# Router tiles over the merged activations, nine expert slots, ten half-megabyte buffers and a written load order in a one-core encoder layer

## The chip, the core and the metric

The program runs on one core of a Trainium2 chip. The core has a matrix engine (PE; its weight loads are shown apart as PEld), a vector engine (DVE), a scalar engine (ACT), GpSimd (POOL) and a sync engine (SP) that here does nothing but issue DMA transfers. The metric is the device time of one execution in microseconds (us). Nearly all of the time goes into streaming weights from HBM once: 616 MB.

## The reference

One layer over 256 tokens of width 2048. Cut to what matters here:

```python
mod = silu(c) @ ada_w + ada_b                    # 2048 -> 6 x 2048
sh1, sc1, g1, sh2, sc2, g2 = split(mod, 6)
h = rmsnorm(x) * (1 + sc1) + sh1
q, k, v, u = split(h @ w_in)                     # 2048 -> 4096
y = gate_na * (attention(q, k, v) @ w_na) + gate_f * (fourier(u) @ w_f)
x = x + g1 * (y @ w_out)                         # w_out: 2048 x 2048, "mow" in the kernel
h = rmsnorm(x) * (1 + sc2) + sh2
group = argmax(h @ wg); two best of 8 experts in that group
x = x + g2 * sum(weight_e * (silu(h @ gate_e) * (h @ up_e)) @ down_e)     # 32 experts, 403 MB
out = rmsnorm(x) * final_g
```

All is float32. The experts' weights ("exw") are 192 pieces of 2 MB (2,097,152 bytes): eight groups ("quads") of four experts, each of 16 pieces gate/up and 8 pieces down.

## The kernel before, in words

**Dense front.** A `section` of a product loads 0.5 MB of weights into one of NW = 8 ring buffers (`load`, L100-104, queue of SP), splits it into a high part on ACT and a low part on DVE (`split`, L106-108) and makes three matmul passes, high with high, high with low, low with high (`t_part`, `n_part`). The high and low parts lie in six 4 KB buffers (`s4`, L89-90). Between the sections, further 0.5 MB loads of `ada2` go through the same ring; each is multiplied on DVE by the conditioning vector and added up (`ada_some`, `mac`, the rows "ada" of DVE). The first stage (L355-379) takes the input projection and half of the gates together with the 64 products of `ada1` (L215). Then come Fourier, output of Fourier, attention (eight 256 KB bias tiles, L495-497), the other gates, the output of attention; there the merged activations arise as `mh`, `ml` (high and low, four tiles each).

**Last dense product ("mow", L618-633).** Four column blocks of 512 with eight sections each. Only here does the code fix the order of SP's queue (`manual_schedule`); elsewhere a scheduler orders the instructions of every engine. In each step the code issues a mow load, then perhaps a quarter (0.5 MB) of one of the first five expert slots (`early_some`, 20 quarters in all, no ring buffer), then perhaps an ada load: 14 of the 23 that remain in the 32 steps (PACE), and nine (`late`) after them. After each column block `residual` (L597-602) multiplies the sum by g1, adds it to x1 and squares it for the norm; `router_part` (L604-616) transposes the new 512 columns of x1 and multiplies them by the router's weights into `plg`.

**Router (L634-702).** Opens new tiles. `lgs` and its neighbours lie at byte 170,880 and after it in each partition, where ring buffers lay before. It copies `plg` into `lgs` (L645-647), sums the squares (`sst`), forms 1/rms, turns the logits with a selecting matmul (`cst`, `lgs`), scales them (`lg`, L656), finds the best group and two experts (`onehot`, L667-674), ranks the tokens (`ma`, `rk`) and builds the 0/1 matrix `gt` that picks 32 tokens for each expert.

**Experts (`quad`, L760-817).** `gather` forms the picked tokens `hq` (`ph`); then each of 24 pieces is multiplied from its slot: 16 into `pg` and `pu`, 8 into `pd`. Pieces lie in slots of 2 MB: five early ones, two more and one that is used once (`NX` = 7, `slot`, `ring` L713-731), so eight at first, seven later, since the one used once becomes the output tile x2. A slot is loaded again, by SP, when PE has used it.

**Tail (L878-918).** The last piece is loaded in four parts; two halves of 256 columns go through `yb`, `po`, the sum with x2 and the square; then 1/rms, scaling and four output transfers.

Of the kernel before, what the change touches and what calls it, by code (L numbers as in the profile page):

```python
# [27 lines left out]
C_ID, C_LT, C_ONE, C_SELR, C_IOTA, C_DESC, C_THR, C_END = 0, 128, 256, 384, 420, 452, 484, 492  # L28
# [4 lines left out]
def const_table():  # L33
# [5 lines left out]
    for j in range(2):  # L39
        t[64 * j + np.arange(36), C_SELR + np.arange(36)] = 1  # L40
# [17 lines left out]
def build(tc, A, out, dbg=None):  # L58
# [15 lines left out]
    wp, _wp = pool("wp", "right", bufs=NW)  # L74
# [14 lines left out]
    def s4(shape, s, dt=F32):  # L89
        return r0.tile(shape, dt, tag="s4", bufs=6, name=nm(s))  # L90
# [8 lines left out]

    def load(src):  # L100

        w = wp.tile([P, 1024], F32, tag="w", name=nm("w"))
        nc.sync.dma_start(w, src)
        return w
# [75 lines left out]
    nc.gpsimd.dma_start(rb, A["rb"])  # L180
# [10 lines left out]
    for i in range(2):  # L191
        crow = wp.tile([P, 1024], F32, tag="w", name=nm("crow"))
# [212 lines left out]
    for i, c in ((0, 1024), (2, 512)):  # L405
        fr = wp.tile([P, 1024], F32, tag="w", name=nm("fr"))
# [5 lines left out]
    zh = rf.tile([P, 2, 258], F32R, name="zh")  # L412
    zl = rf.tile([P, 2, 258], F32R, name="zl")
# [70 lines left out]
    def attention(half):  # L484
# [9 lines left out]
        for i in range(4):  # L494
            bt = rb_.tile([P, 2, 2, P], F32, tag="bias", bufs=2, name=nm("bias"))  # L495
            nc.sync.dma_start(bt, A["rpb"][4 * half + i])
# [38 lines left out]
    _ra.close()  # L535
    mt, _mt = pool("mt", "right")
# [26 lines left out]
    nc.sync.dma_start(x1, A["x"])  # L563
# [20 lines left out]
    nc.vector.tensor_tensor(crow, pc[0:1, 0:36], rb, op=OP.add)  # L584
# [11 lines left out]
    def residual(cb, acs):  # L596
        c = slice(512 * cb, 512 * cb + 512)  # L597
        for tb in range(2):
# [3 lines left out]
            nc.scalar.activation(tmp, x1[:, tb, c], AF.Square, accum_out=ss2[:, tb, cb:cb + 1])  # L602

    def router_part(cb):  # L604
        for pr in range(2):
            px = mps()
            for i in range(2):
                kc = 4 * cb + 2 * pr + i
                for tb in range(2):
                    nc.tensor.transpose(px[:, T * i + P * tb:T * i + P * tb + P],  # L610
                                        x1[:, tb, kc * P:kc * P + P], ident)
            xt2 = s4([P, 2, T], "x1t")
            nc.scalar.copy(xt2, px.rearrange("p (a b) -> p a b", a=2))
            for i in range(2):
# [206 lines left out]
    for go in late:  # L821
        go()
# [172 lines left out]
```

## Time and profile before

| | |
|---|---|
| median of 3 runs | 1600.57 us (1597.12 to 1603.39) |
| the profiled execution | 1598.41 us, of it span 1596.6 us |
| PE, DVE, ACT, POOL busy | 77%, 43%, 22%, 3% |
| moved by DMA | 616.27 MB, mean 386 GB/s |
| chain that ended last | DMA 47%, PE 38%, DVE 5% |

How to read it: busy times are those of one execution; "w<-exw" is a slot (or a ring buffer) filled from the experts' weights; an arrow <- behind an idle time names what ended it. PEclk is the clock that PE was granted, as a share of 2.4 GHz. The dense front lasts to about 642 us, the router to about 670 us, the experts to the end.

### The profile page before, as it was taken

What the parts mean: (1) busy time and instruction counts of PE and PEld (TensorE: products, weight loads), DVE (VectorE), ACT (ScalarE), POOL (GpSimd) and SP (SyncE); (2) the same over time, 40 slices, a digit from 0 to 9 for tenths busy, and PEclk for the clock granted to TensorE, in tenths of its full rate; (3) what the DMA queues carried; (4) which work ended last, traced back from release to release, by engine and by line L of the source; (5) the groups of instructions that cost most, each with busy time, mean ns of one, the idle gap of its engine ahead of it and who ended that gap; (6) DMA issues with size and microseconds to landing.
All of it is one profiled execution on the core that took longest, in us unless ns stands there. A gap on an engine that the chain in (4) does not pass through costs nothing.

```text
span 1596.6 us, 20401 instructions
## 1 busy us (share of the span) xinstructions
PE 1233.2 (77%) x8430; PEld 745.9 (47%) x8430; DVE 679.3 (43%) x946; ACT 349.7 (22%) x535; POOL 43.6 (3%) x40
## 2 busy tenths in 40 slices
PE   4999999999999899679657567667567566556755
PEld 3989999999899777325112112112112112111111
DVE  6989999798887966603003002002002002002002
ACT  3543355444555343112000000000000000000002
POOL 0000000300002100000000000000000000000001
PEclk9999999999999999799889779789779889777878
DMA  9999999899997899699999999999999999999996
GB/s 360 389 337 339 352 359 365 273 328 369 329 346 267 318 409 380 261 427 426 427 426 427 428 427 426 427 426 427 426 427 428 427 427 426 417 427 426 425 428 280
DMA packets 89229, 616.27 MB, mean 386 GB/s; under 512 B 10037, under 2 KB 10341, under 8 KB 64937
## 3 DMA queue, kind: packets, MB, share of 16 engines
q1 hardware_dynamic: 87700, 611.10, 95.2%
q10 hardware_dynamic: 1252, 3.48, 0.6%
q8 instruction: 68, 1.11, 0.3%
q0 software_dynamic: 176, 0.31, 0.1%
q14 instruction: 33, 0.26, 0.0%
HBM read 611.71 MB, written 2.10 MB: 384 GB/s over the span
## 4 chain that ended last, share of the span: by engine, by line
DMA 47%; PE 38%; DVE 5%; issue 1%; ACT 1%; POOL 0%; DVEq 0%; POOLq 0%; ACTq 0%
DMA w<-exw 45%; PE acc L116 23%; PE pd L116 3%; PE m L116 2%; PE ph L116 2%; PE pg L116 2%; PE pu L116 2%; DMA w<-ada 2%; DVE lo L108 1%; DVE ada L223 1%; PE po L116 1%; PE at_u L116 1%; PE pr L116 0%; DVE t L600 0%; PE sp L116 0%
## 5 line engine op out<-in xcount | busy, mean ns | idle before, releaser
L116 PE MATMUL pg<-w,hq 128*32 128x512 f32 x1024 | 185.0, 777 | 217.0 <-DMA w<-exw 217.0
L108 DVE TENSOR_TENSOR lo<-w,hi 128x1024 fp32r<-128x1024 f32 x192 | 239.5, 1253 | 42.6 <-ACT hi L107 37.8
L107 ACT CAST hi<-w 128x1024 fp32r<-128x1024 f32 x192 | 200.8, 1051 | 229.2 <-PE acc L116 179.5
L790 DVE TENSOR_TENSOR act<-act,pu 128x512 f32<-128x512 f32 x8 | 5.5, 688 | 526.2 <-PE pu L116 526.2
L116 PE MATMUL acc<-hh,hi 128*128 128x256 f32 x768 | 212.1, 280 | 0.6 <-ACT hi L107 0.6
L116 PE MATMUL acc<-hl,hi 128*128 128x256 f32 x768 | 211.3, 278 | 0.0
L116 PE MATMUL acc<-hh,lo 128*128 128x256 f32 x768 | 205.7, 279 | 2.2 <-DVE lo L108 2.1
L116 PEld LDWEIGHTS pg<-w,hq 128*32 128x32 f32 x1024 | 25.0, 118 | 363.1 <-DMA w<-exw 345.3
L116 PE MATMUL pu<-w,hq 128*32 128x512 f32 x1024 | 190.0, 793 | 0.0
L223 DVE SCALAR_TENSOR_TENSOR ada<-w,condT,ada 128x1024 f32<-128x1024 f32 x124 | 162.1, 1314 | 13.1 <-DMA w<-ada 12.2
L116 PE MATMUL pd<-w,aT 128*32 128x512 f32 x1024 | 132.2, 630 | 37.0 <-DMA w<-exw 35.5
L116 PEld LDWEIGHTS acc<-hh,hi 128*128 128x128 f32 x768 | 145.3, 189 | 2.1 <-ACT hi L107 1.4
L116 PEld LDWEIGHTS acc<-hl,hi 128*128 128x128 f32 x768 | 145.1, 189 | 0.3 <-issue 0.2
L786 ACT ACTIVATE act<-pg 128x512 f32<-128x512 f32 x8 | 4.8, 597 | 637.3 <-PE pg L116 637.3
L116 PEld LDWEIGHTS acc<-hh,lo 128*128 128x128 f32 x768 | 141.2, 189 | 3.0 <-DVE lo L108 2.6
L116 PE MATMUL po<-yb,gwt 128*128 128x512 f32 (+1 forms) x132 | 75.0, 659 | 30.4 <-DVE yb L808 19.4
L116 PEld LDWEIGHTS pu<-w,hq 128*32 128x32 f32 x1024 | 43.0, 138 | 109.9 <-issue 108.2
L116 PEld LDWEIGHTS ph<-gt,x 128*128 128x128 f32 x512 | 65.2, 195 | 43.8 <-issue 25.6
L116 PEld LDWEIGHTS pd<-w,aT 128*32 128x32 f32 x1024 | 28.7, 112 | 114.7 <-issue 60.4
L215 DVE SCALAR_TENSOR_TENSOR w<-w,condR 128x1024 f32<-128x1024 f32 x64 | 77.7, 1219 | 9.1 <-ACT condR L197 7.4
L116 PE MATMUL ph<-gt,x 128*128 128x128 f32 x512 | 74.8, 288 | 7.1 <-ACT hq L756 3.5
L815 DVE TENSOR_TENSOR x<-x,po 128x512 f32<-128x512 f32 (+1 forms) x66 | 44.3, 671 | 79.8 <-PE po L116 79.8
(246 smaller groups left out, 1481.4 us busy)
## 6 DMA issues: line engine op xcount, KB each, us to landing
w<-exw SPq DMA_DIRECT2D x186, 2048.0 KB, 30.7
w<-ada SPq DMA_DIRECT2D x192, 512.0 KB, 5.8
w<-mixw SPq DMA_DIRECT2D x64, 512.0 KB, 5.6
w<-gatew SPq DMA_DIRECT2D x64, 512.0 KB, 5.4
w<-mow SPq DMA_DIRECT2D x32, 512.0 KB, 10.2
w<-exw SPq DMA_DIRECT2D x24, 512.0 KB, 10.2
w<-fow SPq DMA_DIRECT2D x16, 512.0 KB, 5.3
w<-now SPq DMA_DIRECT2D x16, 512.0 KB, 5.1
```

The source lines that it names most:

```text
L107: nc.scalar.copy(hi, src)
L108: nc.vector.tensor_tensor(lo, src, hi.bitcast(F32), op=OP.subtract)
L116: return nc.tensor.matmul(ps, lhsT, rhs, start=start, stop=stop, skip_group_check=True)
L215: nc.vector.scalar_tensor_tensor(w, w, 1.0, condR[:, 1024 * kh:1024 * kh + 1024], op0=OP.mult, op1=OP.mult, accum_out=dst)
L223: nc.vector.scalar_tensor_tensor(a, w, condT[:, kc:kc + 1], a, op0=OP.mult, op1=OP.add)
L786: nc.scalar.activation(at_[:, 0], pg, AF.Silu)
L790: nc.vector.tensor_tensor(at_[:, 1], at_[:, 0], pu, op=OP.mult)
L815: nc.vector.tensor_tensor(x2[:, tb, c], base[:, tb, c], po[:, 0:n], op=OP.add)
```

## The change

It has these parts:

1. The router's tiles (`rt2`) are opened on the other side of the memory, where `mh` and `ml` lay (bytes 117,216 to 133,696 of each partition); constants that are not needed after the front, and the `s4` tiles, get pools of their own that are closed with the ring.
2. NX is 8: nine expert slots at first, eight later.
3. The ring has ten buffers (NW 8, NQX 2) to the end of the gate sections before the last, eight after.
4. The order of SP's queue is as written from the gates on to the end of mow, not in mow alone. The bias tiles are loaded from GpSimd's queue, the load of x into x1 stands after mow's fifth section.
5. All 23 remaining ada loads go into mow's first 28 steps. Of the 20 early quarters seven go into the steps (one each fourth step), and 13 after the last mow load.
6. The router's logits are computed with tokens on partitions (stationary x1t, 36 columns of `wr`), so that neither `lgs` nor the turning matmul is needed; the very last square moves from ACT to DVE.
7. The experts' weights of the tokens, the row count and the second `gather` are issued after the first `gather`'s last eviction.
8. The last 512 columns of the last quad are multiplied 128 columns at a time, from pieces rearranged on the host; the last piece comes in three parts; only the last 256 columns are multiplied by the final gain after the norm. One output transfer goes through ACT's queue.
9. Tiles are padded so that their addresses agree modulo 64.

The diff, cut to its core:

```diff
-    wp, _wp = pool("wp", "right", bufs=NW)
+    cq, _cq = pool("cq", "right")
+    r4, _r4 = pool("r4", "right")
+    wp, _wp = pool("wp", "right")
+    wq, _wq = pool("wq", "right")
+    rings = [(wp, i) for i in range(NW)] + [(wq, i) for i in range(NW, NW + NQX)]
...
+    def half(s):
+
+        p, i = rings.pop(0)
+        rings.append((p, i))
+        return p.tile([P, 1024], F32, tag=f"w{i}", bufs=1, name=nm(s))
...
+
+    written = ExitStack()
+    written.enter_context(tc.manual_schedule(engines={nc.sync.engine}))
...
-            nc.sync.dma_start(bt, A["rpb"][4 * half + i])
+            nc.gpsimd.dma_start(bt, A["rpb"][4 * half + i])
...
+    rings[:] = [r for r in rings if r[0] is wp]
+    _wq.close()
...
-    nc.sync.dma_start(x1, A["x"])
...
-            nc.scalar.activation(tmp, x1[:, tb, c], AF.Square, accum_out=ss2[:, tb, cb:cb + 1])
+            if cb == 3 and tb:
+                nc.vector.scalar_tensor_tensor(tmp, x1[:, tb, c], 1.0, x1[:, tb, c], op0=OP.mult, op1=OP.mult,
+                                               accum_out=ss2[:, tb, cb:cb + 1])
+            else:
+                nc.scalar.activation(tmp, x1[:, tb, c], AF.Square, accum_out=ss2[:, tb, cb:cb + 1])
 
     def router_part(cb):
+
+        px = [mps() for _ in range(2)]
+        for tb in range(2):
+            for pr in range(2):
+                for i in range(2):
+                    kc = 4 * cb + 2 * pr + i
+                    nc.tensor.transpose(px[pr][:, T * i + P * tb:T * i + P * tb + P],
+                                        x1[:, tb, kc * P:kc * P + P], ident)
         for pr in range(2):
-            px = mps()
+            xt2 = s4([P, 2, T], "x1t")
+            nc.scalar.copy(xt2, px[pr].rearrange("p (a b) -> p a b", a=2))
             for i in range(2):
                 kc = 4 * cb + 2 * pr + i
                 for tb in range(2):
-                    nc.tensor.transpose(px[:, T * i + P * tb:T * i + P * tb + P],
-                                        x1[:, tb, kc * P:kc * P + P], ident)
-            xt2 = s4([P, 2, T], "x1t")
-            nc.scalar.copy(xt2, px.rearrange("p (a b) -> p a b", a=2))
-            for i in range(2):
-                kc = 4 * cb + 2 * pr + i
-                mm(plg[64 * i:64 * i + 36, 0:T], wra[:, kc, :], xt2[:, i, :], kc < 2, kc >= KC - 2)
-
-    with tc.manual_schedule(engines={nc.sync.engine}):
-        for cb in range(4):
-            acs = acc_tiles()
-            for s in range(8):
-                n_part(load(A["mow"][cb, s]), acs, mhf, mlf, 2 * s, s == 0, s == 7)
-                i = 8 * cb + s
-                early_some(max(0, i - 5) * 4 * NA // 26 - max(0, i - 6) * 4 * NA // 26)
-                ada_some((i + 1) * PACE // 32 - i * PACE // 32)
-                if s == 4 and cb:
-                    router_part(cb - 1)
-                if s == 4 and cb == 1:
-
-                    nc.scalar.activation(warm, ones[:, 0:1], AF.Sqrt)
-            if cb == 3:
-                late = [ada_load() for _ in range(len(ada_q))]
-            residual(cb, acs)
+
+                    mm(plg[:, 36 * tb:36 * tb + 36], xt2[:, i, tb * P:tb * P + P], wra[:, kc, :],
+                       kc == 0 and tb == 0, kc == KC - 1)
+
+    left = len(ada_q)
+    for cb in range(4):
+        acs = acc_tiles()
+        for s in range(8):
+            n_part(load(A["mow"][cb, s]), acs, mhf, mlf, 2 * s, s == 0, s == 7)
+            i = 8 * cb + s
+            ada_some(min(left, (i + 1) * left // 28) - (left - len(ada_q)))
+            if i == 4:
+                nc.sync.dma_start(x1, A["x"])
+            if i % 4 == 3 and i > 4:
+                early_some(1)
+            if s == 4 and cb:
+                router_part(cb - 1)
+            if s == 4 and cb == 1:
+
+                nc.scalar.activation(warm, ones[:, 0:1], AF.Sqrt)
+        if cb == 3:
+            early_some(len(quarters))
+        residual(cb, acs)
+    written.close()
...
+    for e in (_mt, _wp, _r4, _cq):
+        e.close()
+
+    rt, _rt2 = pool("rt2", reuse_waits="tile")
     wxb, _wxb = pool("wxb", reuse_waits="tile")
-    rt, _rt2 = pool("rt2", "right")
+    tp, _tp = pool("tp", "right", reuse_waits="tile")
...
-    lgs = rt.tile([P, T], F32, name="lgs")
-    nc.gpsimd.memset(lgs, 0.0)
-    for i in range(2):
-        nc.vector.tensor_copy(lgs[64 * i:64 * i + 36, :], plg[64 * i:64 * i + 36, 0:T])
     sst = rt.tile([P, 2], F32, name="sst")
     nc.vector.tensor_reduce(sst, ss2, axis=AX.X, op=OP.add)
     rs2 = rstd_of(rt, sst, 2)
-    pl = mps()
-    for tb in range(2):
-        mm(pl[:, 36 * tb:36 * tb + 36], lgs[:, tb * P:tb * P + P], cst[:, C_SELR:C_SELR + 36], True, True)
     lg = rt.tile([P, 2, 36], F32, name="lg")
     for tb in range(2):
-        nc.vector.scalar_tensor_tensor(lg[:, tb, :], pl[:, 36 * tb:36 * tb + 36], rs2[:, tb:tb + 1], cbr,
+        nc.vector.scalar_tensor_tensor(lg[:, tb, :], plg[:, 36 * tb:36 * tb + 36], rs2[:, tb:tb + 1], cbr,
                                        op0=OP.mult, op1=OP.add)
...
+            if q == NQ - 1 and cb == 3:
+
+                for k2 in range(2):
+                    w = get(A["exw"][q, KC + 2 * cb + k2], (2048, 4096) if tail is None or k2 == 0 else
+                            (2048, 3072, 4096))
+                    for i in range(2):
+                        c = slice(256 * k2 + 128 * i, 256 * k2 + 128 * i + 128)
+                        for kc in range(4):
+                            for j in range(4):
+                                mm(pd[32 * j:32 * j + 32, c], aT[:, kc * P + 32 * j:kc * P + 32 * j + 32],
+                                   w[4 * i + kc][:, P * j:P * j + P], kc == 0, kc == 3)
+                        if k2:
+                            down(cb, c, pd, yb)
+                    if k2 == 0:
+                        down(cb, slice(0, 256), pd, yb)
+                continue
...
+    behind, first_evict = ExitStack(), last_evict[0]
+    behind.enter_context(tc.issue_after(last_evict[0].ins))
+
+
+    nc.vector.tensor_tensor(ge, gl, gm[:, :, None].to_broadcast([P, 2, 4]), op=OP.subtract)
...
+        with tc.issue_after(first_evict.ins) if q == 0 else ExitStack():
+            hg = gather(q + 1, rk, q % 2)
...
         n = c.stop - c.start
-        nc.scalar.activation(s4([P, 512], "sq")[:, 0:n], x2[:, tb, c], AF.Square, accum_out=ss3[:, tb, i:i + 1])
-        if gain:
+        nc.scalar.activation(temp([P, 512], "sq")[:, 0:n], x2[:, tb, c], AF.Square,
+                             accum_out=ss3[:, tb, parts[tb]:parts[tb] + 1])
+        parts[tb] += 1
+        if c.start < LASTC:
             nc.gpsimd.tensor_tensor(x2[:, tb, c], x2[:, tb, c], fg[:, c], op=OP.mult)
...
-    nc.sync.dma_start(out[:, 0, c0], x2[:, 0, c0])
+    nc.scalar.dma_start(out[:, 0, c0], x2[:, 0, c0])
...
-NW, NX, NA = 8, 7, 5
-
-LEAD, PACE = 3, 14
+NW, NQX, NX, NA = 8, 2, 8, 5
+
+LASTC = 1792
```

What the order of the instructions shows at three places. DVE, around the end of the first column block of mow: t and x are the residual's product and sum, lo the low part of a section, ada an ada product. Before:

```order
L108 TENSOR_TENSOR lo_6467<-w_6464,hi_6466 128x1024
L600 TENSOR_TENSOR t_6483<-acc_6327,g1r_5907 128x512
L601 TENSOR_TENSOR x_6285<-x_6285,t_6483 128x512
L600 TENSOR_TENSOR t_6487<-acc_6328,g1r_5907 128x512
L108 TENSOR_TENSOR lo_6496<-w_6493,hi_6495 128x1024
L601 TENSOR_TENSOR x_6285<-x_6285,t_6487 128x512
L223 SCALAR_TENSOR_TENSOR ada_5950<-w_6531,condT,ada_5950 128x1024
L108 TENSOR_TENSOR lo_6515<-w_6512,hi_6514 128x1024
L108 TENSOR_TENSOR lo_6537<-w_6534,hi_6536 128x1024
L108 TENSOR_TENSOR lo_6555<-w_6552,hi_6554 128x1024
```

After:

```order
L116 TENSOR_TENSOR lo_6483<-w_6480,hi_6482 128x1024
L231 SCALAR_TENSOR_TENSOR ada_5962<-w_6498,condT,ada_5962 128x1024
L612 TENSOR_TENSOR t_6502<-acc_6336,g1r_5919 128x512
L613 TENSOR_TENSOR x_6297<-x_6297,t_6502 128x512
L612 TENSOR_TENSOR t_6506<-acc_6337,g1r_5919 128x512
L231 SCALAR_TENSOR_TENSOR ada_5962<-w_6530,condT,ada_5962 128x1024
L116 TENSOR_TENSOR lo_6515<-w_6512,hi_6514 128x1024
L613 TENSOR_TENSOR x_6297<-x_6297,t_6506 128x512
L116 TENSOR_TENSOR lo_6536<-w_6533,hi_6535 128x1024
L231 SCALAR_TENSOR_TENSOR ada_5962<-w_6569,condT,ada_5962 128x1024
```

One ada product (w_6530) now stands between the second t and the low part of the next block's first section. The same holds at the other two block boundaries.

DVE, from the last residual of mow towards the sum of squares (sst). Before (three more ada products follow, then sst):

```order
L600 TENSOR_TENSOR t_7068<-acc_6869,g1r_5907 128x512
L223 SCALAR_TENSOR_TENSOR ada_5950<-w_7052,condT,ada_5950 128x1024
L600 TENSOR_TENSOR t_7072<-acc_6870,g1r_5907 128x512
L601 TENSOR_TENSOR x_6285<-x_6285,t_7068 128x512
L223 SCALAR_TENSOR_TENSOR ada_5950<-w_7054,condT,ada_5950 128x1024
L601 TENSOR_TENSOR x_6285<-x_6285,t_7072 128x512
L223 SCALAR_TENSOR_TENSOR ada_5950<-w_7056,condT,ada_5950 128x1024
L223 SCALAR_TENSOR_TENSOR ada_5950<-w_7058,condT,ada_5950 128x1024
L223 SCALAR_TENSOR_TENSOR ada_5950<-w_7060,condT,ada_5950 128x1024
```

After:

```order
L612 TENSOR_TENSOR t_7098<-acc_6903,g1r_5919 128x512
L613 TENSOR_TENSOR x_6297<-x_6297,t_7098 128x512
L612 TENSOR_TENSOR t_7102<-acc_6904,g1r_5919 128x512
L613 TENSOR_TENSOR x_6297<-x_6297,t_7102 128x512
L615 SCALAR_TENSOR_TENSOR t_7102,ss_6334<-x_6297 128x512
L675 TENSOR_REDUCE sst<-ss_6334 128x2
```

The eight ada products that stood between and behind the residual's steps are gone from here, and a square (L615) has come.

SP, from the last mow load to the slots. Before, the last mow load and then:

```order
L103 DMA w_7030<-mow 128x1024
L572 DMA w_6297<-exw 128x1024
L103 DMA w_7049<-ada 128x1024
L103 DMA w_7052<-ada 128x1024
L103 DMA w_7054<-ada 128x1024
L103 DMA w_7056<-ada 128x1024
L103 DMA w_7058<-ada 128x1024
L103 DMA w_7060<-ada 128x1024
L103 DMA w_7062<-ada 128x1024
L103 DMA w_7064<-ada 128x1024
L103 DMA w_7066<-ada 128x1024
L727 DMA w_7327<-exw 128x4096
```

After:

```order
L111 DMA w_7066<-mow 128x1024
L584 DMA w_6305<-exw 128x1024 x2
L584 DMA w_6306<-exw 128x1024 x4
L584 DMA w_6307<-exw 128x1024 x4
L584 DMA w_6308<-exw 128x1024 x4
L748 DMA w_7351<-exw 128x4096
L748 DMA w_7361<-exw 128x4096
L748 DMA w_7371<-exw 128x4096
L748 DMA w_7381<-exw 128x4096
L748 DMA w_7391<-exw 128x4096
```

The nine ada loads stand ahead of the 2 MB slots (128x4096) in the kernel before; now 14 quarters of early slots stand there, the first of them that of the last step, and a fourth 2 MB slot follows directly.

## Rows read from the trace of the kernel before

**Rows 1.** The page: shares of the chain of waits by engine.

```profile
DMA 47%; PE 38%; DVE 5%; issue 1%; ACT 1%; POOL 0%; DVEq 0%; POOLq 0%; ACTq 0%
```

**Rows 2.** Windows by stage: start:end, length, busy per engine, granted clock, DMA share, GB/s.

```profile
0.00:100.00 100.00, 79.00 (x562) 71.51 (x563) 81.76 (x139) 49.04 (x63) 1.47 (x6) 0.97 0.97 369
100.00:230.00 130.00, 123.70 (x984) 118.93 (x983) 124.40 (x173) 51.27 (x56) 0.00 (x0) 0.97 0.95 346
520.00:554.00 34.00, 29.64 (x220) 26.12 (x220) 34.00 (x31) 12.42 (x12) 5.98 (x2) 1.00 0.87 316
554.00:620.00 66.00, 63.05 (x287) 49.16 (x286) 42.25 (x42) 26.84 (x37) 0.00 (x0) 1.00 1.02 407
620.00:642.00 22.00, 21.70 (x102) 17.00 (x100) 13.37 (x13) 7.13 (x8) 0.00 (x0) 1.00 0.98 359
642.00:656.00 14.00, 4.94 (x20) 2.81 (x20) 13.34 (x23) 4.11 (x8) 0.31 (x1) 0.58 1.00 415
...
692.00:1576.00 884.00, 585.96 (x3528) 171.51 (x3520) 100.96 (x201) 43.92 (x92) 5.04 (x4) 0.85 1.01 426
```

**Rows 3.** Windows around the router, same columns.

```profile
656.00:660.00 4.00, 0.00 (x0) 0.00 (x0) 3.59 (x23) 0.41 (x2) 0.00 (x0) 0.50 0.06 25
660.00:670.00 10.00, 7.65 (x42) 5.34 (x43) 5.32 (x30) 0.82 (x2) 0.74 (x2) 0.59 0.01 3
670.00:672.00 2.00, 2.00 (x20) 1.06 (x22) 0.41 (x1) 0.46 (x1) 0.00 (x0) 1.00 0.69 160
```

**Rows 4.** Timeline of the router: start, length, engine, instruction, idle before and its releaser.

```profile
641.31 0.39 PE L116 MATMUL acc<-lo,mh 128*128 128x512 f32 x1
...
645.63 7.26 DVE L223 SCALAR_TENSOR_TENSOR ada<-w,condT,ada 128x1024 f32<-128x1024 f32 x6
...
647.40 1.93 PE L116 MATMUL plg<-x1t,wr 128*36 128x256 f32 x8
653.00 0.31 POOL L645 MEMSET lgs<- 128x256 f32 x1 [102.79 <-DVE ada L223]
...
655.48 0.42 DVE L656 SCALAR_TENSOR_TENSOR lg<-m,rr,cbr 128x36 f32<-128x36 f32 x2 [0.30 <-PE m L116]
...
667.49 1.40 PE L116 MATMUL pg<-w,hq 128*32 128x512 f32 x8
...
668.71 1.03 PE L116 MATMUL pu<-w,hq 128*32 128x512 f32 x8
```

**Rows 5.** The page: groups of DVE, mean ns of one.

```profile
L108 DVE TENSOR_TENSOR lo<-w,hi 128x1024 fp32r<-128x1024 f32 x192 | 239.5, 1253 | 42.6 <-ACT hi L107 37.8
L223 DVE SCALAR_TENSOR_TENSOR ada<-w,condT,ada 128x1024 f32<-128x1024 f32 x124 | 162.1, 1314 | 13.1 <-DMA w<-ada 12.2
```

**Rows 6.** Waits of PE in mow: total us, times, longest.

```profile
PE acc L116 <- DVE lo L108: 0.9, 3, 0.3
```

**Rows 7.** Tile x: issue of the x1 load in SP's queue, first and last start.

```profile
L563 SPq DMA_DIRECT2D x<-x x1: 328/328/328, 550.2 to 550.2; - x1
```

**Rows 8.** Landing of tile bias by SP's queue, then of ada_b_row by GpSimd's queue.

```profile
DMA to landing us min/median/max: 3.5/4.7/5.9
...
DMA to landing us min/median/max: 2.7/2.9/3.0
```

**Rows 9.** Timeline of the tail.

```profile
1581.12 1.05 PE L116 MATMUL pd<-w,aT 128*32 128x512 f32 x4 [0.21 <-DMA w<-exw]
1582.28 0.76 DVE L808 TENSOR_TENSOR yb<-pd,g2r 128x256 f32<-128x256 f32 x2 [5.64 <-PE pd L116]
1582.76 2.35 PE L116 MATMUL po<-yb,gwt 128*128 128x256 f32 x8 [0.58 <-DVE yb L808]
...
1585.63 0.40 ACT L890 ACTIVATE sq<-x 128x256 f32<-128x256 f32 x1
...
1586.16 0.16 DVE L897 TENSOR_REDUCE sst<-ss 128x2 f32<-128x10 f32 x1 [0.60 <-ACT sq L890]
...
1588.64 0.35 SPq L910 DMA_DIRECT2D out<-x  x1
```

More of the change, by code (lines that the diff above doesn't have):

```diff
@@ L89, in s4 @@
     def s4(shape, s, dt=F32):
[L90 removed]
+        return r4.tile(shape, dt, tag="s4", bufs=6, name=nm(s))
     turn = [1]
@@ L716, in ring, with get @@
         todo, there = list(order) + list(once), list(there)
-        def get(src, parts=1):
+        def get(src, ends=(4096,)):
             if not todo:
@@ L724, in get @@
                 w = slot(i)
-                n = 4096 // parts
-                for i in range(parts):
-                    eng.dma_start(w[:, n * i:n * i + n], src[:, n * i:n * i + n])
+                for i, e in zip((0,) + ends, ends):
+                    eng.dma_start(w[:, i:e], src[:, i:e])
             return [w[:, 512 * j:512 * j + 512] for j in range(8)]
@@ L793, in quad, with down @@
             nc.tensor.transpose(pt[:, kc * P:kc * P + P], at_[:, 1, kc * P:kc * P + P], ident)
-        aT = s4([P, 512], "aT")
+        aT = temp([P, 512], "aT")
         nc.scalar.copy(aT, pt)
+        def down(cb, c, pd, yb):
+            o = slice(512 * cb + c.start, 512 * cb + c.stop)
+            n = c.stop - c.start
+            nc.vector.tensor_tensor(yb[:, c], pd[:, c], g2r[:, o], op=OP.mult)
+            for tb in range(2):
+                if tail is None:
+                    po = pe.tile([P, 512], F32, tag="po", bufs=1, name=nm("po"))
+                else:
+                    po = pe.tile([P, 512], F32, tag="ph", bufs=2, name=nm("po"))
+                mm(po[:, 0:n], gwt[:, tb * P:tb * P + P], yb[:, c], True, True)
+                nc.vector.tensor_tensor(x2[:, tb, o], base[:, tb, o], po[:, 0:n], op=OP.add)
+                if tail is not None:
+                    tail(x2, tb, o)
         for cb in range(4):
             pd = pe.tile([P, 512], F32, tag="pd", bufs=2, name=nm("pd"))
+            yb = temp([P, 512], "yb", 2)
+            if q == NQ - 1 and cb == 3:
[13 more added lines that the diff above has]
+                continue
             for k2 in range(2):
-                w = get(A["exw"][q, KC + 2 * cb + k2], 4 if tail is not None and cb == 3 and k2 else 1)
+                w = get(A["exw"][q, KC + 2 * cb + k2])
                 for kc in (2 * k2, 2 * k2 + 1):
@@ L854, in build @@
     show("rk", rk)
+    behind.close()
     for q in range(NQ - 1):
```

80 lines of the change are left out of this document (32 added, 48 removed).

## The prediction

> **What bounds the kernel now.** I read the chain of waits first. It is shared by DMA (47%) and PE (38%) [rows 1], which are two stages, not a mixture: the windows by stage show PE nearly always busy until about 642 us (63.05 of 66 us in the greater part of the product called mow, 21.70 of 22 in the rest), and from 692 us on DMA at 426 GB/s while PE is idle a third of the time [rows 2]. So the second half is worth just the bytes that it still has to move: a 2 MB piece (2.097 MB) takes 2.097/0.426 = 4.92 us, and nothing that PE does there matters before the last piece.
>
> Between the stages lies what the change is aimed at. The windows around the router show DMA busy for 6% of 656 to 660, 1% of 660 to 670 and 69% of the next 2 us [rows 3]: idle for 3.8 + 9.9 + 0.6 = 14.3 us, from about 656.2 to 670.6. All eight slots are full and none can be loaded again before the router has let PE use the first. The timeline says why the router is late [rows 4]. The last mow matmul ends at 641.31 + 0.39 = 641.7, which I call T. The logits `plg` are done at 647.40 + 1.93 = 649.3. Yet POOL clears `lgs` only at 653.00, having waited for DVE's ada products, whose last run of six lasts to 652.9: `lgs` lies where those late loads were. From the scaled logits (655.48) to the first expert matmul (667.49) it is 12.0 us, and 2.25 us more until the first `pu` ends (668.71 + 1.03) and its slot is free; DMA follows 0.9 us later.
>
> **The change part by part.** *Router.* The new order of DVE has five instructions of about 0.69 us between the last matmul and `sst` (the square 512 wide like the others) where there were four and eight ada products. The first starts 0.9 us before T, when its half of the sum is complete, as in the kernel before; so `sst` at T + 2.6. The logits follow the second sum of x1 (T + 1.9) by transposes, a copy and products, which took from 645.03 + 0.68 = 645.7 to 649.3, 3.6 us: T + 5.5 (the trace has no row for products with 36 columns; between nothing and the 1.93 us of the present form, so T + 3.6 to T + 5.5, and I take the late end, which is the nearest row's). 12.0 us later, less 0.6 for the transposes of `gt` that now stand behind the gather, is the first expert matmul: T + 16.9; the first slot is free at T + 19.2 and DMA could move into it at T + 20.1.
>
> *What DMA has to do until then.* From 554 to 656 us DMA moved 66 x 407 + 22 x 359 + 14 x 415 = 40.6 MB [rows 2]. What mow and the first eight slots need in all is 55 ring loads and 20 quarters of 0.524 MB, x1 (2.1) and three slots (6.3): 47.7 MB, so 7.1 MB had come before 554, of which about 1.6 MB was x1, issued at 550.2 [rows 7]. The changed kernel loads x1 later and one slot more: 47.7 + 2.1 - 5.5 = 44.3 MB from 554 on. At 410 GB/s, all but the four big slots (35.9 MB) is through at 554 + 87.6 = 641.6, that is at about T. The big slots lie over `mh`, `ml` and the ring, so the first of them can go only after the last matmul, say T + 1.2 with the same lag of some 0.9 us. Four slots take 8.39/0.42 = 20.0 us: nine slots are full at T + 21.2. That is behind T + 20.1, so no gap is left, with a margin of only 1 us. Before, the ninth piece was complete at 670.6 + 4.9 = 675.5 = 641.7 + 33.8. The gain is 33.8 - 21.2 = 12.6 us, less whatever T moves.
>
> *T itself.* The order shows one ada product more between the residual's second t and the low part of the next block's first section, at each of three block boundaries. Before, PE waited at them for 0.9 us in all [rows 6], so there is no slack to swallow it: 3 x 1.28 (the product's duration in rows 4, 7.26/6 = 1.21 at the least, 1.31 in the mean of all [rows 5]) = 3.8 us. Bounds: 0, if the scheduler's order leaves DVE ahead, to 6 us, if each delay also makes a ring load late. I take 3.8. Inside a block DVE has 8 low parts of 1.25, 6.6 ada of 1.31 and four residual steps of 0.69 = 21.4 us [rows 5] to 22 us of PE, so it just holds. Router and ninth slot together: 12.6 - 3.8 = 8.8 us.
>
> *Ten buffers and the written order* in the front: I count nothing. From 100 to 230 us DVE is busy 124.4 of 130 us, and from 520 to 554 all the time [rows 2]; a buffer more doesn't shorten DVE's work. Bounds: a gain of the PE idle time there, 6.3 + 4.4 us, and a loss under the rivals. *Bias tiles on GpSimd's queue*: hidden, since each is loaded two ahead; behind a late one stand POOL's add, DVE's sum `sb` and, in DVE's order, the low parts that PE needs. *Tokens' weights after the gather*: needed only at `pt`, which in the new order comes after the gather; nothing. *Padding, addresses*: no row shows an effect of them; nothing. Had it 1% of the 884 us at 426 GB/s in it [rows 2], that would be 9 us either way, which the range holds.
>
> *Tail.* From the arrival of the last part (1581.12) to `sst` it is 5.04 us: four products of 512 columns 1.05, then two halves one behind the other [rows 9]. Now half the columns' work follows the last arrival (eight products of 128 columns, about 0.5), and one block of 128 through `yb`, `po`, the sum and the square, which at 0.3 to 0.4 us a step and two token halves is about 2.8 us. That is 1.7 us less if half a microsecond goes to queueing; bounds 0.8 and 2.4. The output transfers start that much earlier.
>
> Sum: 8.8 + 1.7 = 10.5 us off the profiled execution's 1598.41 (span 1596.6 and 1.8 around it): 1587.9. That execution lies 2.2 us below the median of the runs shown; a new median may lie at either, and I take 1589.
>
> **Rivals.** *The gain is lost in mow* (1598). All 23 ada loads and 28 mow loads now share eight ring buffers with seven quarters in 28 steps: 1.82 ring loads a step where there were 1.44. If loads come late or DVE's 21.4 us don't fit, each block loses 2 to 3 us more, T moves by 12 and the gain is about nil. For it: DVE at full load. Against it: DMA at 407 GB/s with PE waiting 0.9 us [rows 2, 6]. Chance 0.15.
>
> *The front gains too* (1581): the PE idle time above goes, or T doesn't move. For it: two more buffers let loads arrive earlier. Against: DVE is the fuller engine. Chance 0.15.
>
> *The first stage starves* (about 1612, the slower side). Before the gates the scheduler still orders SP, and where its queue followed the code before, loads now stand up to five places from there. DVE and PE are both 95% busy from 100 to 230 us, so a wrong load that holds a buffer stops both. Were PE only as busy there as in the first 100 us (79%), the 123.7 us would take 157 [rows 2], 27 us more than 130; 22 of that gives 1611. It decides from 19 us of added idle time; less only cancels the gain. Against it: ten buffers cover five places. Chance 0.10.
>
> *Bias tiles come late* (1599). The row: two small transfers from GpSimd's queue landed after 2.7 to 3.0 us, eight bias tiles by SP's after 3.5 to 5.9 [rows 8]; the former fell amid DVE work, so nothing shows lateness. If each tile came one DVE instruction late, 1.25 to 1.31 us [rows 5], and DVE and then PE stood for it, eight would cost 10 us. Chance 0.06. The Trainium skill, "SBUF — State Buffer", section "SBUF: two separate sides", speaks for this rival: transfers issued by GpSimd get their descriptors from its cores, which are shut out while DVE runs a certain fast form of instruction. By that rule the sum would end near the 1599 above; the trace's landings do not bear it out so far.
>
> **How the numbers follow.** My own case has 0.54 and a range of 1584 to 1595; it puts nine tenths of itself under 1592.6. The bound for "same" is 0.5%, 8 us, about what a measurement of this kernel can tell. Faster: 0.49 + 0.15 = 0.64. Slower: 0.10. Same: the rest, 0.26. The range is 1579 to 1600: it leaves out the starving front and the better half of the front's gain.
>
> **What would show it.** Right: DMA without a gap after mow, at 425 GB/s from the last quarter on; `sst` within 3 us of the last mow matmul, the first expert matmul 17 us after it; three waits of PE for a low part of 1.3 us more each; 3.3 us in place of 5.0 from the last arrival to the last `sst`. Wrong: a gap of some us after the ninth slot (the router later than T + 21); PE idle in the first 230 us above the 27 us of now; DVE waiting for bias tiles; T more than 6 us later.

## The result and the profile after

The changed kernel takes 1612.6 us (median of 8 runs, 1607.64 to 1615.87) against 1601.5 us (8 runs, 1597.12 to 1604.05) of the kernel before: ratio 1.0064, 95% interval 1.0047 to 1.0080. It is slower, by 11 us; 1589 was forecast. The profiled execution took 1615.24 us with a span of 1613.4 us, so 16.8 us of span are to be found. Single executions of one kernel differ by some us (this one is 2.6 us above its median, the profiled one of the kernel before 3.1 us below its own), so 5.7 of the 16.8 are the spread of executions. A difference in T of under some 3 us between two versions says little without their medians.

The chain of waits of the changed kernel, shares by engine, beside [rows 1]: DMA and PE have both grown.

```profile
DMA 50%; PE 42%; DVE 5%; ACT 1%; issue 1%; POOL 0%; SPq 0%; DVEq 0%; ACTq 0%; POOLq 0%
```

The router of the changed kernel: first the windows (columns as in [rows 2]), then the timeline, where [rows 3] and [rows 4] had the gap.

```profile
671.00:680.00 9.00, 3.26 (x24) 2.70 (x24) 6.95 (x31) 1.90 (x5) 0.00 (x0) 0.80 1.03 429
680.00:692.00 12.00, 9.94 (x54) 6.07 (x58) 2.72 (x11) 1.26 (x3) 0.51 (x2) 0.58 1.00 423
692.00:700.00 8.00, 8.00 (x75) 3.38 (x70) 0.82 (x2) 0.94 (x3) 0.00 (x0) 1.00 1.00 418
720.00:1590.00 870.00, 580.12 (x3472) 168.67 (x3471) 99.86 (x200) 43.12 (x90) 5.01 (x4) 0.85 1.01 427
```

```profile
670.24 0.39 PE L124 MATMUL acc<-lo,mh 128*128 128x512 f32 x1
...
673.12 0.16 DVE L675 TENSOR_REDUCE sst<-ss 128x2 f32<-128x8 f32 x1
...
675.51 0.42 DVE L679 SCALAR_TENSOR_TENSOR lg<-plg,rr,cbr 128x36 f32<-128x36 f32 x2 [0.49 <-PE plg L124]
...
687.02 1.94 PE L124 MATMUL pg<-w,hq 128*32 128x512 f32 x8
```

DMA never stops now: 429, 423 and 418 GB/s where 14.3 us were empty. From T, the end of the last mow matmul, `sst` is at T + 2.5, the logits at T + 4.9, the first expert matmul at T + 16.4. But T is 670.24 + 0.39 = 670.6, not 641.7: 28.9 us later. The experts' last bytes land at 1596.8 us, before at 1580.7, so only 16.1 of the 28.9 us are left by then: router and ninth slot gave back 12.8. From there to the end of the span it is 16.7 us, before 16.0. 28.9 - 12.8 + 0.7 = 16.8.

Where T went is seen in PE's own rows. The page's group of one product form of the front, before, then after (busy us, mean ns of one):

```profile
L116 PE MATMUL acc<-hh,hi 128*128 128x256 f32 x768 | 212.1, 280 | 0.6 <-ACT hi L107 0.6
```

```profile
L124 PE MATMUL acc<-hh,hi 128*128 128x256 f32 x768 | 216.1, 284 | 1.6 <-ACT hi L115 1.6
```

The rows give each of these products 280 ns, although one starts every 114 to 119 ns: they overlap, so the pace is read from the distance between the starts. PE's timeline of the changed kernel, and below it that of a version (the first of the experiments) that differs from it by 16 unused columns in a table of constants; in both, the last row shown is sixteen products behind the first:

```profile
499.74 0.28 PE L124 MATMUL acc<-hh,lo 128*128 128x256 f32 x1
499.86 0.28 PE L124 MATMUL acc<-hh,hi 128*128 128x256 f32 x1
499.98 0.28 PE L124 MATMUL acc<-hl,hi 128*128 128x256 f32 x1
...
501.64 0.28 PE L124 MATMUL acc<-hh,hi 128*128 128x256 f32 x1
```

```profile
499.73 0.28 PE L124 MATMUL acc<-hh,hi 128*128 128x256 f32 x1
499.85 0.28 PE L124 MATMUL acc<-hl,hi 128*128 128x256 f32 x1
499.96 0.28 PE L124 MATMUL acc<-hh,lo 128*128 128x256 f32 x1
...
501.55 0.28 PE L124 MATMUL acc<-hl,hi 128*128 128x256 f32 x1
```

(501.64 - 499.74)/16 = 118.8 ns against (501.55 - 499.73)/16 = 113.8 ns, both at the full clock. Over all the 256-column products of the front the mean distance is 114.2 ns before and 118.8 ns after; with some 3600 of them that is about 17 us of PE, which hardly waits there. Mow's 512-column products stand 228 ns apart in both kernels. In the first stage, PE is as busy as in [rows 2] and gets less done, 959 products recorded where there were 984:

```profile
0.00:100.00 100.00, 77.36 (x515) 69.65 (x516) 78.16 (x135) 46.77 (x61) 1.46 (x6) 0.95 0.96 362
100.00:230.00 130.00, 125.05 (x959) 121.33 (x958) 122.36 (x171) 50.11 (x56) 0.00 (x0) 0.97 0.94 347
```

### The profile page after: what moved, and what is told of

It reads as the page before. It is cut to its first block, busy times and chain, and to the rows that moved or that the text cites. A ratio compares the mean times of both kernels' runs of the same rounds, so it can differ in the third digit from the quotient of the medians.

```text
span 1613.4 us, 20624 instructions
## 1 busy us (share of the span) xinstructions
PE 1258.1 (78%) x8558; PEld 774.5 (48%) x8558; DVE 684.0 (42%) x949; ACT 349.5 (22%) x537; POOL 52.0 (3%) x49
## 4 chain that ended last, share of the span: by engine, by line
DMA 50%; PE 42%; DVE 5%; ACT 1%; issue 1%; POOL 0%; SPq 0%; DVEq 0%; ACTq 0%; POOLq 0%
DMA w<-exw 46%; PE acc L124 27%; PE pd L124 3%; PE m L124 3%; PE pg L124 2%; PE pu L124 2%; PE ph L124 2%; DVE lo L116 2%; DMA w<-ada 1%; PE at_u L124 1%; DVE w L223 1%; ACT hi L115 1%; PE po L124 1%; DMA w<-mixw 1%; DMA w<-mow 1%
## 5 line engine op out<-in xcount | busy, mean ns | idle before, releaser
L124 PE MATMUL acc<-hh,hi 128*128 128x256 f32 x768 | 216.1, 284 | 1.6 <-ACT hi L115 1.6
L124 PE MATMUL acc<-hl,hi 128*128 128x256 f32 x768 | 215.3, 283 | 0.0
L124 PE MATMUL acc<-hh,lo 128*128 128x256 f32 x768 | 209.4, 283 | 0.0
L231 DVE SCALAR_TENSOR_TENSOR ada<-w,condT,ada 128x1024 f32<-128x1024 f32 x124 | 165.7, 1344 | 16.2 <-DMA w<-ada 15.9
L124 PE MATMUL pd<-w,aT 128*32 128x512 f32 (+1 forms) x1120 | 132.8, 599 | 41.1 <-DMA w<-exw 40.8
L124 PE MATMUL po<-yb,gwt 128*128 128x512 f32 (+2 forms) x136 | 73.3, 629 | 30.7 <-DVE yb L821 20.0
L828 DVE TENSOR_TENSOR x<-x,po 128x512 f32<-128x512 f32 (+2 forms) x68 | 44.5, 656 | 85.2 <-PE po L124 85.2
```

The costliest lines, as they stand in the source:

```text
L124: return nc.tensor.matmul(ps, lhsT, rhs, start=start, stop=stop, skip_group_check=True)
L231: nc.vector.scalar_tensor_tensor(a, w, condT[:, kc:kc + 1], a, op0=OP.mult, op1=OP.add)
L828: nc.vector.tensor_tensor(x2[:, tb, o], base[:, tb, o], po[:, 0:n], op=OP.add)
```

## The experiments

In each, T is the end of the last mow matmul and the ratio is to the kernel before, run on the same chip.

**Where two tiles begin (R against A and O).** The front's products have `hh` or `hl` moving and the split weights (`s4`) stationary. In the kernel before `hh` begins at byte 39,072 of a partition (32 modulo 128), in the changed one at 34,912 (96); the `s4` tiles begin at 96 modulo 128 in both. Four kernels move the one, the other, or both by 64 bytes and leave the instructions alone; all tiles of a side move together, and only the distances 0 and 64 bytes occur.

```diff
 e1_left64, changed kernel, hh to 32:            C_END  472 -> 488
 e2_before_left64, kernel before, hh to 96:      C_END  492 -> 508
 e3_right64, changed kernel, s4 to 32:           rb = cq.tile([1, 48]) -> [1, 64]
 e4_both64, changed kernel, hh to 32, s4 to 32:  both
```

> The changed kernel with its constants table 64 bytes longer per partition, so that all tiles on the left side (hh, hl, yfh, ath, x1, the early slots) begin 64 bytes later: hh at 32 modulo 128 in place of 96. No instruction and no order differs. Theory A (the pace of the 256-column matmuls hangs on where the moving tile begins modulo 128): their spacing falls from 118.7 to about 113.3 ns, the last mow matmul from 670.6 to about 649 us, the time from 1612.6 to about 1590 us. Theory R (it hangs on moving and stationary tile agreeing modulo 128): the same here. Rival O (the order of the matmuls sets the pace): 118.7 ns stays, 1612 us.

> The kernel before with its constants table 64 bytes longer, so that hh begins at 96 modulo 128 in place of 32. Theories A and R: spacing from 113.3 to 118.7 ns, last mow matmul from 641.7 to about 663 us, time from 1601 to about 1622 us. Rival O: no change, 1601 us.

> The changed kernel with one tile on the right side 64 bytes longer: the split weights (hi, lo) begin at 32 modulo 128 in place of 96, hh stays at 96. Theory R (agreement of the two): 113.3 ns, about 1590 us. Theory A (the moving tile alone): 118.7 ns for the products that move hh, 1612 us; the products that move hi and lo (mow, now at 113.5 ns for 256 columns) would also change, faster or slower by 5%. Rival O: 118.7 ns, 1612 us, mow the same.

> The changed kernel with both sides shifted: hh and the split weights both at 32 modulo 128. Theory A: 113.3 ns, about 1590 us. Theory R: 118.7 ns, 1612 us, since both agree again. Rival O: 1612 us.

Measured: e1 1600.5 us, ratio 0.9998 (0.9986 to 1.0009), T 655.4; e2 1614.9, 1.0084 (1.0067 to 1.0101), T 658.1; e3 1600.4, 0.9992 (0.9981 to 1.0002), T 656.9; e4 1614.2, 1.0076 (1.0059 to 1.0092), T 666.8. The same group of e1 and of e2:

```profile
L124 PE MATMUL acc<-hh,hi 128*128 128x256 f32 x768 | 212.1, 279 | 1.3 <-ACT hi L115 1.3
```

```profile
L116 PE MATMUL acc<-hh,hi 128*128 128x256 f32 x768 | 216.7, 285 | 0.4 <-ACT hi L107 0.4
```

The fast pace goes with e1 and e3, where the two places differ modulo 128, the slow one with e2 and e4, where they agree; neither place does it by itself, and not the order, since e2 has the order of before. R holds for the pace. It had named too large a gain and loss: 1590 us for e1 and e3, measured 1600.5 and 1600.4; 1622 for e2, measured 1614.9. The 64 bytes alone make the kernel before 13.5 us slower. The rest was studied on e1, which is still no faster than the kernel before.

**The written order and the x1 load (W, X), the last block, the ninth slot.**

```diff
 f1_written_mow: e1, written order of SP's queue from mow on only
 f2_x1_pool:     e1, - nc.sync.dma_start(x1, A["x"])  + nc.gpsimd.dma_start(x1, A["x"])
 f4_old_tail:    e1, last 512 columns, LASTC and the parts of the last piece as before
 f5_eight_slots: e1, NX 8 -> 7
 g8_written_all: e1, written order from the first load on
```

> As e1_left64 (matmuls at the fast pace, last mow matmul at 655.4, 13.7 us behind the kernel before), but the order of SP's queue is as written in mow alone, as in the kernel before; from the gates to mow the scheduler orders it again. Theory W (the written order makes the queue stand still: in e1_left64 it waited from 505.2 to 523.1 for a ring buffer that an ada load held, while loads of the next section stood behind): that standstill falls to about half, the first mow matmul comes 5 to 10 us earlier than 548.4, time about 1590 to 1595 us. Rival D (DVE, busy all the time from 517 to 560 in both kernels, sets this stage's length whatever the queue does): first mow matmul at 548, time 1600 us.

> As e1_left64, but the load of x into x1 is issued from GpSimd's queue in place of SP's. Theory X (in SP's queue this load waited about 8 us for POOL's last sum, with mow loads behind it: DMA at 53 GB/s from 550 to 555 and PE and DVE idle from 560 on): SP doesn't stand still there, the last mow matmul is 3 to 6 us earlier than 655.4, time about 1595 to 1597 us. Rival: the loads behind it had slack, the same time, 1600 us.

> As e1_left64, but the last 512 columns are computed as in the kernel before (last piece in four parts, products of 512 columns, two halves of 256 columns). Theory P (the new tail is a chain of PE and DVE steps in which each block's po stands before the next block's products, so that it ends later after the last byte than the old one: 17.2 us from the end of the last slot's transfer to the end, against 16 before): 1 to 3 us faster than 1600.5, that is about 1598. The prediction's step (new tail 1.7 us shorter): 1602.

> As e1_left64, but with NX 7, that is eight slots at first and seven later. The prediction's account of the ninth slot (nine slots are full 1 us after the first could be released): with eight, DMA stands still some 3 to 5 us while the router ends, time 1604 to 1606 us. Rival: the slots are filled late enough anyway that no gap opens, 1600 us.

> As e1_left64, but SP's queue is in written order from the first load on, not only from the gates. The prediction's rival of a starving first stage put the displaced order there: were it a cause, the gates' end would come earlier by some us and the time fall below 1598 us. Rival: the first stage is set by DVE and the pace of PE, 1600 us.

Measured: f1 1607.2 (1.0041, 1.0025 to 1.0057), T 663.1; f2 1601.7 (1.0002, 0.9989 to 1.0015), T 656.7; f4 1600.1 (0.9994, 0.9980 to 1.0008); f5 1603.7 (1.0019, 1.0007 to 1.0031); g8 1606.4 (1.0025, 1.0013 to 1.0038), T 662.5. W and X fell as sole causes. f1 and g8 missed both their expectations: a written order that begins later or earlier than at the gates costs 6 to 7 us here. The old last block can't be told from the new one, nor in g3 below. Without the ninth slot the gap is back, 326 GB/s where e1 has 420:

```profile
660.00:680.00 20.00, 13.45 (x82) 7.62 (x86) 7.00 (x31) 1.74 (x4) 0.51 (x2) 0.66 0.81 326
```

and the slot is worth 3.2 us (f5 1603.7, just under its 1604 to 1606) with the earlier router in place. What the earlier router is worth alone wasn't measured; it would be most of the 12.8 if the two simply add.

**The pace of the ada products (P), the ring.** The change puts an ada load behind nearly every mow load. g2 sets counts by hand, none in the steps around a block's end; g6 takes the two extra buffers away.

```diff
 g2_pace: e1,
-            ada_some(min(left, (i + 1) * left // 28) - (left - len(ada_q)))
+            ada_some((0, 0, 1, 0, 1, 0, 1, 0, 0, 0, 2, 2, 1, 1, 1, 0, 0, 0, 2, 2, 1, 1, 1, 0, 0, 0, 2, 1, 1, 1, 1, 0)[i])
 g3_pace_old_tail: g2 with f4's last block
 g6_ring8: e1, NW, NQX 8, 2 -> 8, 0
```

> As e1_left64, but the 23 ada loads of mow are paced otherwise: three in the first column block (as in the kernel before; e1_left64 has six or seven) and none at a block boundary, so that DVE's order there is again t, x, t, low part. Theory P (what e1_left64 still loses to the kernel before up to the last mow matmul, 655.4 against 641.7 us, comes from ada products moved forward into a stretch where DVE is full, and to the boundaries): first block of mow 27.0 to about 25 us, second and third 27.1 to 25.5, last mow matmul at about 647 to 649, time about 1593 to 1595 us. Rival: DVE has the same work in all and the delay only moves within mow: last mow matmul at 655, time 1600 us.

> As g2_pace, with the last 512 columns as in the kernel before. If the two are independent: g2_pace's time less 0 to 2 us. This is the candidate for the fastest version: about 1592 us by theory P, 1599 by its rival.

> As e1_left64, but with eight ring buffers from the start (NQX 0). The prediction counted nothing for ten: 1600 us. Rival B (two more buffers keep PE and DVE supplied): the last mow matmul 3 us or more later than 655.4, time 1603 us or more.

Measured: g2 1600.3 (0.9988, 0.9976 to 1.0000), T 655.8; g3 1601.4 (0.9998, 0.9986 to 1.0010); g6 1597.3 (0.9973, 0.9961 to 0.9986), T 652.4. Theory P had T at 647 to 649 in g2 and fell: the pace did shorten mow's second to fourth block from 27.1, 27.1 and 25.9 us (e1) to 25.8, 25.9 and 24.6, and the first grew from 27.0 to 30.2, so the delay only moved. g3, forecast 0 to 2 us faster than g2, was 1.1 slower. g6 was faster than either of its expectations: the ten buffers cost 3.2 us, and without them the stage before mow takes 76.1 us in place of 79.4. From 500 to 600 us SP's longest stand at an ada load, which waits for a ring buffer that DVE must first read, is 17.4 us with ten buffers (e1) and 11.7 with eight (g6); why it is longer with more buffers was not isolated.

```profile
SPq L111 <- DVE ada L231: 30.0, 16, 17.4
```

```profile
SPq L111 <- DVE ada L231: 28.4, 19, 11.7
```

**Addresses, buffers, pace and x1 load together, and each taken out again (S, Q, V, Q2).** Why did the first block grow? In g2, from 540 to 560 us, DMA moved 207 GB/s. SP stood for 9.7 us at the x1 load, which waits for the last gate tile `g`, and every mow load behind it in the written order stood too.

```diff
 h5_ring8_pace:      g6 with g2's pace
 h1_ring8_pace_x1:   h5, x1 load on GpSimd's queue (as f2)
 i1_ring8_x1:        h1 without the pace
 i2_ten_pace_x1:     h1 with ten buffers
 i3_best_right:      h1, C_END 488 -> 472 (hh back to 96, agreeing)
 h2_front_as_before: g6, order written in mow only, x1 load ahead of mow on SP
```

> Eight ring buffers throughout (as in g6_ring8) and the 23 ada products paced around the block boundaries (as in g2_pace). Theory S (the two gains are separate: the ring's 3 us in the attention-output section, the boundaries' 1.3 us each in the last dense product): the last matmul of that product ends at 648 to 650 us, ratio to before 0.995 to 0.997, time 1593 to 1597 us. Rival Q (the work that a pace moves from the boundaries waits elsewhere, since DVE and the queue of SP have the same sum): the end stays at 652 to 653 us, first block 28 to 30 us long, ratio 0.997 to 0.999.

> As h5_ring8_pace, and the load of x into x1 goes through GpSimd's queue, not through SP's written order. Theory S: without a wait of SP at that load (7.6 us in the changed kernel's trace) the first block of the last dense product falls below 27 us, its last matmul ends at 645 to 648 us, ratio 0.993 to 0.996. Rival Q: the wait of SP was covered by loads already in the ring, so the end is within 1 us of h5_ring8_pace's and the ratio within 0.001 of it.

> Eight ring buffers throughout, SP's order written in the last dense product alone, and x1 loaded ahead of it, all as in the kernel before; the ada products still as the change has them. Theory S (ring, order and x1 load carry what the stages before the last dense product lost): its first matmul comes at 541 to 543 us as before (542), its end lies at 648 to 650 us, 3 boundaries of 1.3 us and the denser ada products behind before's 642, ratio 0.994 to 0.997. Rival Q (the order in which the scheduler places the loads there is the worse one with this tile layout, as f1_written_mow was slower by 6.7 us with ten buffers): end at 656 us or later, ratio above 1.

> Eight ring buffers and the x1 load on GpSimd's queue, the ada products crowded as in the change (h1_ring8_pace_x1 without its pace). Theory V (the ring's refill behind the x1 load is the price, the pace is worth little): the end of the last dense product at 643 to 646 us, ratio 0.994 to 0.996. Rival Q2 (the x1 load is worth something only if the ada products are paced, since with them crowded DVE is late in the first block anyway, as the run with ten buffers showed): the end within 1 us of g6_ring8's 652 us, ratio 0.997 to 0.998.

> h1_ring8_pace_x1 with the two extra ring buffers back. Theory V: with paced ada products and the x1 load out of SP's order, the ten buffers cost their 3 us and no more: the end at 645 to 646 us, ratio 0.995 to 0.996. Rival Q2: with ten buffers DVE or SP stands still longer after the attention-output section (17 us there), which keeps the first block at 27 us or more: the end at 649 us or later, ratio 0.997 to 1.0.

> h1_ring8_pace_x1 with the left tiles put 64 bytes back, so that hh and the split weights begin at the same place modulo 128 again (96). Theory R (the agreement slows each 256-column product by some 5 ns, whatever stands around it): the end of the last dense product 12 to 16 us later than h1's 642, ratio 0.999 to 1.004. Rival (the slower products are hidden once DMA, SP and DVE are less in the way): within 5 us of h1, ratio below 0.997.

| | us | ratio, interval | T |
|---|---|---|---|
| g6 (neither pace nor x1) | 1597.3 | 0.9973, 0.9961 to 0.9986 | 652.4 |
| h5 (pace) | 1598.2 | 0.9979, 0.9967 to 0.9992 | 650.2 |
| i1 (x1) | 1595.4 | 0.9960, 0.9944 to 0.9976 | 653.3 |
| **h1 (both)** | **1589.9** | **0.9931, 0.9913 to 0.9949** | **642.5** |
| i2 (h1, ten buffers) | 1593.8 | 0.9947, 0.9928 to 0.9966 | 647.0 |
| i3 (h1, tiles agree) | 1598.0 | 0.9983, 0.9970 to 0.9996 | 650.5 |
| h2 | 1595.9 | 0.9974, 0.9958 to 0.9989 | 653.8 |

SP's queue around the x1 load, h5 and then h1. In h5 the load starts at 552.48, after 11.1 us of waiting for `g`, and no mow load starts from 541 to 552; in h1 they go on.

```profile
538.63 1.52 SPq L111 DMA_DIRECT2D w<-mow  x2
540.96 0.33 SPq L111 DMA_DIRECT2D w<-ada  x1
552.48 0.33 SPq L647 DMA_DIRECT2D x<-x  x1
552.90 0.86 SPq L111 DMA_DIRECT2D w<-mow  x2
```

```profile
539.95 0.33 SPq L111 DMA_DIRECT2D w<-ada  x1
541.15 2.60 SPq L111 DMA_DIRECT2D w<-mow  x2
544.55 0.33 SPq L111 DMA_DIRECT2D w<-ada  x1
548.08 0.33 SPq L111 DMA_DIRECT2D w<-mow  x1
```

Who paid for it: the waits of SP in h5 from 500 to 600 us, the waits of PE in h5's first mow block (total us, times, longest), and DVE's group there with its idle time.

```profile
SPq L647 <- POOL g L556: 11.1, 1, 11.1
```

```profile
PE acc L124 <- ACT hi L115: 5.2, 1, 5.2
```

```profile
L116 DVE TENSOR_TENSOR lo<-w,hi 128x1024 fp32r<-128x1024 f32 x8 | 9.6, 1216 | 7.1 <-ACT hi L115 6.9
```

In h1 that block has neither wait and takes 23.0 us (h5 29.9). The pace and the x1 load act only together. By the medians, against g6: pace alone 0.9 us slower, x1 alone 1.9 faster, both 7.4 faster. With ten buffers it is the same: against e1 (1600.5) the pace alone is 0.2 faster (g2), x1 alone 1.2 slower (f2), both 6.7 faster (i2). T comes 2.2 us earlier by the pace alone, 0.9 later by x1 alone, 9.9 earlier by both. With the ada products crowded DVE has six of them in the first block (9.8 us, h1 three, 6.0 us): the block takes 29.1 us where the loads come late (g6) and still 27.6 where they come in time (i1). With them spread the loads are what is late.

The verdicts are mixed. By T, V fell (it had T at 643 to 646 in i1, without the pace) and Q2 was nearer, but i1's ratio is V's 0.994 to 0.996 and not Q2's 0.997 to 0.998; i1's profiled execution is the slowest of its nine. For i2, T lies between V's 645 to 646 and Q2's 649, and the two buffers cost 4.5 us of it, 3.9 by the medians. h1 came earlier than S had it, at S's ratio. h5 has S's T, at the edge, but Q's ratio and Q's long first block. h5's 2.2 us of T did not shorten its time: the experts' last bytes land at 1579.0 us, in g6 at 1578.4. The versions with g2's pace still have 395.2 to 395.7 MB to move at T, those without it 393.7 to 393.8, so the pace is partly paid for behind T; where the added bytes come from was not isolated.

The agreement cost 8.0 us in i3, not 12 to 16, nor under 5: both expectations missed. All of it arises before mow (first mow matmul at 550.9 us in i3, at 542.9 in h1; mow takes 99.5 us in both). The window of h1 and then of i3 shows where the difference to the other pairs lies: in the first stage i3 records as many products as h1, both beside a DVE that is busy 125 of 130 us.

```profile
100.00:230.00 130.00, 125.00 (x996) 119.72 (x995) 125.14 (x174) 52.01 (x57) 0.00 (x0) 1.00 0.95 354
```

```profile
100.00:230.00 130.00, 127.51 (x1004) 122.67 (x1003) 125.46 (x176) 52.10 (x57) 0.00 (x0) 1.00 0.96 358
```

At about 248 us i3 is only 1.5 us behind h1, where the changed kernel is 6.3 behind e1 and e2 5.8 behind the kernel before. Why the slow products fit in there and not in the others is not shown; the clock differs too (0.97 in the changed kernel, 1.00 in h1 and i3). h2 missed both its expectations: by its ratio it can't be told from g6. Its profiled execution is 4.9 us above its median, so its T says little; in that one trace the stage before mow ends 7 us later than in g6 and the first block is about 3 us shorter, so the written order in the front and the place of the x1 load may cancel, which one trace doesn't show.

## Why the prediction was wrong, step by step

- **The step that failed: "Padding, addresses: no row shows an effect of them; nothing".** The range allowed 9 us for addresses, but in the stage that DMA bounds (426 GB/s then, 427 now: no effect). The effect lies in the front, on PE: T 670.6 with agreement, 655.4 without (e1), 12 us of the time (1612.6 and 1600.5). The argument "a buffer more doesn't shorten DVE's work" looked at DVE alone where PE was as full (123.70 and 124.4 of 130 us in [rows 2]); a step of PE that grows by 4% can show there at once. It need not: in i3 most of it stayed hidden in that stage.
- **T + 3.8 us** was 28.9. After the addresses (15.2) 13.7 remain. The boundaries are about right: PE's waits for the low part there, in place of [rows 6], below, 3.9 - 0.9 = 3.0 us, against the 3.8 forecast. ([rows 6] begins at 554; with the block before that the kernel before has 3.1 us in five waits.) Missing were the ten buffers (3.0 here, 4.5 in i2 against h1), counted as nothing, and the x1 load in the written order, whose waiting followers weren't counted though a moved step was to be priced with its queue; with the pace, which also takes away the boundaries' 3.0, it is 9.9 us. These edits (addresses, buffers, pace with x1 load) bring T from 670.6 by 655.4 and 652.4 to 642.5, 0.8 us behind the kernel before. The split depends on the order in which they are taken out (i1 to i3).

```profile
PE acc L124 <- DVE lo L116: 3.9, 3, 1.3
```

- **Router and ninth slot, 12.6**: right for the changed kernel, 12.8 measured, with `sst`, logits and first expert matmul within 0.6 us of T + 2.6, T + 5.5 and T + 16.9, and no gap. It hung on how much was loaded by T: in h1, with its added bytes behind T, the last bytes land 931.3 us after T, before 939.0, a gain of 7.7 only.
- **Tail, 1.7 off**: wrong in sign, 0.7 on. (The forecast's 0.5 and 2.8 us are 3.3, which is 1.7 under 5.04 with nothing left for queueing.) After the last bytes had landed (1596.8) two blocks of 128 columns were still to be done, not one, since PE was behind:

```profile
1595.75 1.13 PE L124 MATMUL po<-yb,gwt 128*128 128x256 f32 x4 [0.55 <-DVE yb L821]
...
1596.82 1.08 PE L124 MATMUL pd<-w,aT 128*32 128x128 f32 x32
...
1598.95 1.08 PE L124 MATMUL pd<-w,aT 128*32 128x128 f32 x32
...
1602.22 0.17 DVE L945 TENSOR_REDUCE sst<-ss 128x2 f32<-128x12 f32 x1 [0.73 <-ACT sq L936]
```

Each block is a chain `pd`, `yb`, `po`, sum of 2.1 us on PE and DVE, and none of these rows waits for DMA. In h1 PE does wait for the last part, and from there to `sst` it is 1577.00 - 1574.16 = 2.84 us, under the 3.3 forecast:

```profile
1574.16 0.64 PE L124 MATMUL pd<-w,aT 128*32 128x128 f32 x16 [0.43 <-DMA w<-exw]
...
1577.00 0.17 DVE L945 TENSOR_REDUCE sst<-ss 128x2 f32<-128x12 f32 x1 [0.74 <-ACT sq L936]
```

The working was right for a PE that keeps up; it is not sure to. No run isolates what decides that, but the traces differ in two things. In h1 32 of the 64 products `pd` of the last block's first half stand ahead of the `po` before them; in the changed kernel and in e1 that `po` comes first. And the changed kernel's granted clock was 0.50 from 1588 to 1590 (columns as in [rows 2]), after PE had been idle for 2.9 us; in h1 it was 1.00 after the same idle time. e1, at the full clock, was behind as well:

```profile
1588.00:1590.00 2.00, 2.00 (x12) 0.22 (x4) 0.00 (x0) 0.00 (x0) 0.00 (x0) 0.50 0.92 379
```

- **The rivals.** *The first stage starves* named 1612 and hit the time by chance: PE was idle for 27.6 us in the first 230 us, before 27.3. *Lost in mow* had the right place for a part: mow took 108.0 us (562.6 to 670.6) where it took 100.2, 7.8 of the 12 us that this rival put on T. *Bias tiles late*: not what cost the time. `bias` landed after 5.8 us in the median (4.7 before); POOL's add waited for it, 17.5 us in four waits, but DVE's `sb` waited for PE alone (5.3 us). So this case's trace shows no cost on the path of the rule of the Trainium skill, "SBUF — State Buffer", section "SBUF: two separate sides", that transfers issued by GpSimd can be held up by DVE. *The front gains* found no support.

## What to carry to other kernels

A change that moves tiles moves their starting bytes: compare the distance between consecutive matmuls of one form before looking for waits, since a slower pace leaves no idle time behind. A written queue order makes every load that waits for a buffer a stop for all behind it: try such a load on another queue, and look at what is late next, since here it gained only with the ada products spread out too. Two fixes that seem worthless alone (0.9 us slower, 1.9 faster) can be worth 7 us together, so take them out of the best version, not only put them into the worst.

## What had not been expected of the hardware

The front's 256-column products whose two tiles begin at the same byte modulo 128 stood 118.6 to 119.8 ns apart in the mean (four kernels), the others 114.2 to 115.4 (all kernels without agreement), at the full clock and with no wait where the rows above show them. Only distances of 0 and 64 bytes were tried. The 512-column products of mow took 227 to 228 ns, the fast pace column for column (114 ns for 256), although their two tiles agreed too, at 96 in both kernels and at 32 in e3. The front's own 512-column products with `hh` or `hl` don't show the cost either: 229 to 230 ns without agreement (before, e1, e3), 227 to 232 with it (changed kernel, e2, e4). Why the agreement costs the one form and not the other is open.
